# Low parts of the left pieces on VectorE instead of GpSimd, in the down stage of a decoder layer

## The chip, the cores and the metric

The kernel is one program on one core of a Trainium2 chip. The metric is the time of one execution on the device in microseconds, read as the median of several runs. The core has five engines with a queue each, which run their own instructions in order: TensorE (PE: matmuls, and PEld: loads of the weight operand), VectorE (DVE), ScalarE (ACT), GpSimd (POOL), and SyncE (SP), which here only issues DMAs.

## The reference, cut to what matters

The whole is one decoder layer in float32 on 1024 tokens of width 1024: an entry normalisation, two groups of attention heads, an output projection, a normalisation, a SwiGLU feed-forward of width 2816, and a last normalisation. The change touches the last product of the feed-forward, the one with w_down:

```
def swiglu_ffn(h, w_gate_up, w_down):
    gate, up = jnp.split(h @ w_gate_up, 2, axis=-1)
    return (jax.nn.silu(gate) * up) @ w_down
...
        ffn = swiglu_ffn(h, w_gate_up[l], w_down[l])
        h = layer_norm(ALPHA * h + ffn, ln2_g[l], ln2_b[l])
```

## The kernel before, in words

**Precision.** TensorE multiplies in a reduced form of float32. To keep the precision, every operand is split into a high part (a cast, on ScalarE) and a low part (operand minus high part, a subtraction of two tiles in SBUF on VectorE or GpSimd). Each product is then three matmuls: high x high, high x low, low x high. `split_to` (L766 to L769) does one split; its argument `eng` is the engine of the low part.

**The down stage.** The product of the activations (1024 x 2816) with w_down (2816 x 1024) is done as a 2 x 2 block product with seven instead of eight block multiplications, named P1, P5, P2, P3, P6, P7, P4 in the order in which they run. Each block multiplication has 11 steps k of 128 rows (KF = 11), and each step needs one left piece (128 x 512, from `a_dram`, which the stage before has filled with the four blocks and three sums of them) and one right piece (128 x 512, a block of w_down or a sum of blocks). `left_part` (L811) loads a left piece into a tile `ar` and splits it into `ahl`; `right_part` (L816) forms block sums of the right pieces in place (tiles `bq`, L818) and splits into `bhl`, or for P7 and P4 into another `bq`. `down` (L771) multiplies the pair: four blocks of 128 tokens x three matmuls, 12 matmuls in all (L776), into four PSUM tiles `pd`. The tags ahl and bhl have four buffers each, ar eight.

The first four steps of P1 (EARLY, L784) stand apart, run while the stage before is still ending, and split into tiles `w`; the code of the other steps of P1 is the loop over k from 4 to 10, and that of P5, P2, P3, P6, P7, P4 the loop at L868. After a block multiplication VectorE adds the PSUM tiles into the rows `h` (`scaled`, L849, h<-h,pd); P1's result goes through a tile `uu` and is added from there (h<-h,uu). After P6 and P4 the function `one` normalises finished rows and stores them.

**Who does what.** Before the change GpSimd takes the low parts of all left pieces (L768, ahl and, in every other step of P7 and P4, bhl) and one block sum of P3 (L818); VectorE takes the low parts of all right pieces, the other block sums (one in P5, two in P6, L818), and all drains; ScalarE takes all casts (L767).

**What sets the order.** The instructions are put in order by a scheduler, engine by engine, when the program is built; so an instruction may stand well ahead of the place where the code issues it, and the order on each engine is fixed from then on. The loads of the down stage are on SyncE's queue in the order of the code (`Ordered`). The tail of the stage before leaves four more sums on GpSimd (L712 to L715), behind which ScalarE issues stores to `a_dram` (L716 to L718).

Of the kernel before, what the change touches and what calls it, by code (L numbers as in the profile page):

```python
# [74 lines left out]
def layer(ctx: ExitStack, tc: tile.TileContext, x, ln_in, w_sw, w_sb, norm_g,  # L75
          sinks, rel_bias, onehot, w_out, ln1, w_gu, w_down, ln2, out):
    nc = tc.nc
    pe, act, dve, pool = nc.tensor, nc.scalar, nc.vector, nc.gpsimd
# [38 lines left out]
    def ln_stats(xt, n=2):  # L117
        bst = st.tile([P, n, 6], F32, tag=f"bst{n}", name="bst")
        w = D // n
        for i in range(n):  # L120
            dve.bn_stats(out=bst[:, i, :], in_=xt[:, i * w:(i + 1) * w])
        mv = st.tile([P, 2], F32, tag="mv", name="mv")
        dve.bn_aggr(out=mv, in_=bst)
        rstd = st.tile([P, 1], F32, tag="rstd", name="rstd")
        rpow(rstd, mv[:, 1:2], 1.0, LN_EPS)
        return mv[:, 0:1], rstd

    def ln_apply(dst, xt, g, b, fast=False):
        mu, rstd = ln_stats(xt)
        if fast:  # L130
            dve.scalar_tensor_tensor(out=dst, in0=xt, scalar=mu, in1=g, op0=ALU.subtract, op1=ALU.mult)
            for i in range(2):
                h = slice(i * 512, i * 512 + 512)
                dve.scalar_tensor_tensor(out=dst[:, h], in0=dst[:, h], scalar=rstd, in1=b[:, h],
                                         op0=ALU.mult, op1=ALU.add)
            return
        nmu = st.tile([P, 1], F32, tag="nmu", name="nmu")
        dve.tensor_scalar(out=nmu, in0=mu, scalar1=-1.0, scalar2=None, op0=ALU.mult)
        for i in range(2):
            h = slice(i * 512, i * 512 + 512)  # L140
            act.activation(dst[:, h], xt[:, h], AF.Identity, bias=nmu)
            dve.scalar_tensor_tensor(out=dst[:, h], in0=dst[:, h], scalar=rstd, in1=g[:, h],
                                     op0=ALU.mult, op1=ALU.mult)
            pool.tensor_tensor(out=dst[:, h], in0=dst[:, h], in1=b[:, h], op=ALU.add)
# [621 lines left out]
    def split_to(w, src, eng):  # L766
        act.copy(w[:, 0], src)  # L767
        eng.tensor_tensor(out=w[:, 1], in0=src, in1=_f(w[:, 0]), op=ALU.subtract)  # L768
        return w  # L769

    def down(pd, k, a, b, first, end, ts=range(4)):  # L771
        for t in ts:
            tok = slice(t * P, t * P + P)
            n = 0
            for x, y in ((a[:, 0, tok], b[0]), (a[:, 0, tok], b[1]), (a[:, 1, tok], b[0])):
                pe.matmul(pd[t], x, y, start=(first and k == 0 and n == 0),  # L776
                          stop=(end and k == KF - 1 and n == 2), skip_group_check=True)
                n += 1

    def down_banks(tags):  # L780
        return [bps.tile([P, 512], F32, tag=tags[t // 2], name="pd") for t in range(4)]
# [5 lines left out]
    for k in range(EARLY):  # L787
        r = fw.tile([P, 2, 512], F32, tag="gr", bufs=2, name="r")
# [11 lines left out]
    def raw_b(k, i):  # L800
        return bq[k + i // 2 * KF][:, i % 2 * 512:i % 2 * 512 + 512]

    def load_b(k, i):
        h = slice(i % 2 * 512, i % 2 * 512 + 512)
        f = k + i // 2 * KF
        sp.dma_start(raw_b(k, i), w_down[f * P:(f + 1) * P, h])

    def parts(tag, src, eng, pl=dr, bufs=4):
        return split_to(pl.tile([P, 2, 512], F32R, tag=tag, bufs=bufs, name=tag), src, eng)

    def left_part(i, k, tag="ahl"):  # L811
        r = dr.tile([P, 512], F32, tag="ar", bufs=8, name="ar")
        sp.dma_start(r, a_dram[k][:, i])
        return parts(tag, r, pool)

    def right_part(name, k):  # L816
        b11, b12, b21, b22 = (raw_b(k, i) for i in range(4)) if name != "P1" else [raw_b(k, 0)] * 4
        sub = lambda eng, dst, x, y: eng.tensor_tensor(out=dst, in0=x, in1=y, op=ALU.subtract)  # L818
        if name == "P5":
            sub(dve, b11, b12, b11)  # L820
        elif name == "P6":
            sub(dve, b11, b22, b11)
        src = {"P1": b11, "P5": b11, "P6": b11, "P2": b21, "P3": b22, "P7": b12, "P4": b21}[name]
        if name in ("P7", "P4"):
            w = parts("bq", src, dve, *((dr, KF + 1) if name == "P7" else (dn, KF + 2)))
        else:
            w = parts("bhl", src, dve)
        if name == "P3":
            sub(pool, b12, b22, b12)
        elif name == "P6":  # L830
            sub(dve, b21, b21, b11)
        return w[:, 0], w[:, 1]
# [9 lines left out]
    with tc.tile_pool(name="dn", bufs=4, reuse_waits="tile") as dn:  # L842
        bq += [dn.tile([P, D], F32, tag="bq", bufs=KF + 2, name="bq") for k in range(KF)]
        h = [dn.tile([P, D], F32, tag="h", bufs=NT, name="h") for t in range(NT)]
        LEFT = {"P2": 1, "P4": 2, "P5": 3, "P6": 4, "P7": 5, "P3": 6}
        NEEDS = {"P5": (1,), "P2": (2,), "P3": (3,), "P6": (), "P7": (), "P4": ()}

        def scaled(dst, src, c=1.0):
            dve.scalar_tensor_tensor(out=dst, in0=dst, scalar=c, in1=src, op0=ALU.mult, op1=ALU.add)  # L849

        def one(t):
            ot = dn.tile([P, D], F32, tag="ot", bufs=2, name="ot")
            rows = slice(t * P, (t + 1) * P)
            if t < NT - 1:
                ln_apply(ot, h[t], g2, b2)
                nc.sync.dma_start(out[rows, :], ot)
                return
            mu, rstd = ln_stats(h[t], 4)
            for x in (d0, d1):
                dve.scalar_tensor_tensor(out=ot[:, x], in0=h[t][:, x], scalar=mu, in1=g2[:, x],  # L860
                                         op0=ALU.subtract, op1=ALU.mult)
            for x, q in ((d0, act), (d1, nc.sync)):
                dve.scalar_tensor_tensor(out=ot[:, x], in0=ot[:, x], scalar=rstd, in1=b2[:, x],  # L863
                                         op0=ALU.mult, op1=ALU.add)
                q.dma_start(out[rows, x], ot[:, x])

        pt = down_banks(("pp", "tr"))
        for name in ("P5", "P2", "P3", "P6", "P7", "P4"):  # L868
            if name == "P6":
                pz = down_banks(("z", "av"))  # L870
            ps = pt if name in ("P5", "P3") else pz
            first, last, end = name in ("P5", "P6"), name == "P4", name in ("P2", "P4", "P3")
            held = []
            for k in range(KF):
                if name == "P5" and k < EARLY:
                    load_b(k, 0)
                for i in NEEDS[name]:
                    load_b(k, i)
                if name == "P5" and k > KF - 5:
                    for t in (k - KF + 8, k - KF + 4):  # L880
                        sp.dma_start(h[t], h1_dram[t])
                ab = (left_part(LEFT[name], k, "bhl" if name in ("P7", "P4") and k % 2 else "ahl"), right_part(name, k))
                if last and k > 3:
                    held.append((k, *ab))
                else:
                    down(ps, k, *ab, first, end)
            if name == "P3":
                g2 = dn.tile([P, D], F32, tag="g2", bufs=1, name="g2")
                b2 = dn.tile([P, D], F32, tag="b2", bufs=1, name="b2")
                bc_load(g2, ln2[0])  # L890
                bc_load(b2, ln2[1])
            for t in range(4):
                for k, a, b in held:
                    down(ps, k, a, b, first, end, (t,))
                if name == "P5":
                    scaled(h[4 + t][:, d1], ps[t], ALPHA)
                elif name == "P2":
                    scaled(h[t][:, d0], ps[t], ALPHA)
                elif name in ("P3", "P6"):
                    scaled(h[t][:, d1], ps[t])  # L900
                elif name == "P7":
                    scaled(h[4 + t][:, d1], ps[t])
                else:
                    scaled(h[4 + t][:, d0], ps[t])
                if name in ("P6", "P4"):
                    one(t if name == "P6" else 4 + t)
            if name == "P2":
                for t in range(4):
                    scaled(h[t][:, d1], uu[:, t], ALPHA)
                    scaled(h[4 + t][:, d0], uu[:, t], ALPHA)  # L910
                    scaled(h[4 + t][:, d1], uu[:, t])
# [50 lines left out]
```

## Time and profile before

| | us |
|---|---|
| median of 3 runs | 1236.27 |
| lowest and highest run | 1234.16, 1238.58 |
| the profiled execution's own time | 1236.33 |
| its span, first to last instruction | 1234.6 |
| TensorE busy | 1151.2 (93%) |
| VectorE busy | 867.5 (70%) |
| GpSimd busy | 750.0 (61%) |
| ScalarE busy | 570.9 (46%) |
| TensorE's mean granted clock | 0.964 |

The shares are means over the whole layer; the change lies in the last fifth of it, so views of that stretch alone are read below. Times in the rows are microseconds from the span's start. A group's idle time is that of the engine just before the instructions, with the engine whose work ended it.

### The profile page before, as it was taken

The numbers are of one execution on the slowest core, as the hardware profiler recorded it, in microseconds if no ns is written. First come the engines' busy times: TensorE is split into PE (matmuls) and PEld (weight loads), VectorE is DVE, ScalarE is ACT, GpSimd is POOL, SyncE is SP. The second block draws the span as 40 slices with busy tenths as digits, with TensorE's granted clock in tenths as the row PEclk, the third lists the DMA queues.
The fourth block names the chain that finished last, engine by engine and source line by source line (L and its number), as shares of the span: only waits on it lengthen the run. The fifth ranks groups of instructions, "written<-read, shape, count | busy, mean of one in ns | idle before, by whom it ended". The sixth has DMA issues, their size and how long they took to land. (4 is left out here: it accounts for less than half of the span.)

```text
span 1234.6 us, 17707 instructions
## 1 busy us (share of the span) xinstructions
PE 1151.2 (93%) x6246; PEld 990.9 (80%) x6246; DVE 867.5 (70%) x1257; ACT 570.9 (46%) x1224; POOL 750.0 (61%) x682
## 2 busy tenths in 40 slices
PE   5698999999998998977999999999999999979997
PEld 4688999899997886765888888888888888757785
DVE  7885786787889894777765645656456349998645
ACT  4565677767678564233433222332232234425531
POOL 5514344556647877567877656666557455774694
PEclk9798999999999898987999999999999999989998
DMA  7213102020105525134333323333323269643441
GB/s 274 93 55 94 35 23 77 23 66 22 49 18 172 186 99 192 73 121 145 119 128 111 103 76 112 111 111 102 95 94 111 95 218 396 212 137 93 114 134 68
DMA packets 60054, 140.69 MB, mean 114 GB/s; under 512 B 7060, under 2 KB 18877, under 8 KB 59966
## 3 DMA queue, kind: packets, MB, share of 16 engines
q1 hardware_dynamic: 45406, 110.71, 28.1%
q10 hardware_dynamic: 14560, 28.85, 6.1%
q8 instruction: 49, 0.80, 0.3%
q14 instruction: 39, 0.32, 0.1%
HBM read 95.75 MB, written 41.17 MB: 111 GB/s over the span
## 5 line engine op out<-in xcount | busy, mean ns | idle before, releaser
L107 POOL TENSOR_TENSOR w<-s,w 128x512 fp32r<-128x512 f32 x88 | 124.1, 1413 | 119.2 <-ACT w L106 119.2
L154 PE MATMUL pp<-xh,whi 128*128 128x256 f32 x544 | 158.8, 293 | 0.0
L154 PE MATMUL pp<-xh,wlo 128*128 128x256 f32 x544 | 158.2, 291 | 0.0
L154 PE MATMUL pp<-xl,whi 128*128 128x256 f32 x544 | 157.5, 290 | 0.0
L776 PE MATMUL pd<-bhl,ahl 128*128 128x512 f32 x612 | 146.6, 400 | 10.0 <-DVE bhl L768 9.6
L776 PEld LDWEIGHTS pd<-bhl,ahl 128*128 128x128 f32 x612 | 117.0, 193 | 39.4 <-DVE bhl L768 14.9
L106 ACT CAST w<-s 128x512 fp32r<-128x512 f32 x88 | 54.4, 622 | 202.7 <-PE pgu L703 118.9
L768 POOL TENSOR_TENSOR ahl<-ar,ahl 128x512 fp32r<-128x512 f32 x63 | 92.6, 1477 | 59.1 <-ACT ahl L767 57.0
L735 DVE TENSOR_TENSOR t<-t,pgu 128x512 f32<-128x512 f32 x88 | 60.1, 683 | 96.6 <-PE pgu L703 96.2
L433 POOL TENSOR_TENSOR s<-s,s 128x127 f32<-128x127 f32 (+2 forms) x96 | 92.6, 969 | 37.7 <-DVE s L429 33.3
L154 PEld LDWEIGHTS pp<-xh,wlo 128*128 128x128 f32 x544 | 106.6, 196 | 1.2
L154 PEld LDWEIGHTS pp<-xl,whi 128*128 128x128 f32 x544 | 106.6, 196 | 1.0
L154 PEld LDWEIGHTS pp<-xh,whi 128*128 128x128 f32 x544 | 106.5, 196 | 0.6
L429 DVE TENSOR_TENSOR_SCAN s<-s,brk 128x128 f32<-128x128 f32 (+1 forms) x64 | 74.7, 1174 | 11.2 <-ACT s L420 10.6
L374 POOL TENSOR_TENSOR L<-L,rd 128x512 f32<-128x512 f32 (+1 forms) x32 | 30.9, 989 | 81.5 <-DVE rd L372 63.9
L110 ACT CAST at<-tra 128x256 fp32r<-128x256 f32 (+1 forms) x160 | 55.5, 356 | 52.7 <-DVE at L111 30.9
L768 DVE TENSOR_TENSOR bhl<-bq,bhl 128x512 fp32r<-128x512 f32 x51 | 67.8, 1338 | 8.2 <-ACT bhl L767 7.9
L111 DVE TENSOR_TENSOR at<-tra,at 128x256 fp32r<-128x256 f32 (+1 forms) x160 | 58.5, 383 | 15.8 <-ACT at L110 14.6
L107 POOL TENSOR_TENSOR w<-gr,w 128x512 fp32r<-128x512 f32 x44 | 61.2, 1405 | 2.3 <-ACT w L106 2.3
L703 PE MATMUL pgu<-B11h,w 128*128 128x512 f32 x176 | 59.1, 398 | 1.4 <-ACT w L106 1.4
L767 ACT CAST ahl<-ar 128x512 fp32r<-128x512 f32 x63 | 38.9, 619 | 43.0 <-POOL ahl L768 17.1
L703 PE MATMUL pgu<-T4h,w 128*128 128x512 f32 x176 | 57.9, 390 | 0.0
(222 smaller groups left out, 3351.2 us busy)
## 6 DMA issues: line engine op xcount, KB each, us to landing
ar<-a_dram SPq DMA_DIRECT2D x73, 256.0 KB, 2.9
a_dram<-act ACTq DMA_DIRECT2D x33, 512.0 KB, 2.6
gr<-in_w_gu SPq DMA_DIRECT2D x24, 512.0 KB, 3.6
ur<-in_w_gu SPq DMA_DIRECT2D x23, 512.0 KB, 3.5
bq<-in_w_down SPq DMA_DIRECT2D x44, 256.0 KB, 4.3
raw<-in_w_sb SPq DMA_DIRECT2D x12, 512.0 KB, 3.4
h_dram<-x ACTq DMA_DIRECT2D x8, 512.0 KB, 3.3
m<-o_dram SPq DMA_DIRECT2D x32, 128.0 KB, 3.0
```

What stands on the lines that cost most here:

```text
L106: act.copy(hi, raw)
L107: pool.tensor_tensor(out=lo, in0=raw, in1=_f(hi), op=ALU.subtract)
L110: act.copy(hi, ps)
L111: dve.tensor_tensor(out=lo, in0=ps, in1=_f(hi), op=ALU.subtract)
L154: pe.matmul(ps, a, b, start=(i == 0), stop=(i == n - 1))
L429: dve.tensor_tensor_scan(s2[:, 0:w][:, ::-1], s2[:, 0:w][:, ::-1], brk[:, 512 - w:][:, ::-1] if last else zero.broadcast_to([P, w]), 1.0 i ...
L433: pool.tensor_tensor(out=s1[:, 0:m], in0=s1[:, 0:m], in1=s2[:, 1:m + 1], op=ALU.mult)
L703: pe.matmul(ps, a, b, start=(start and n == 0), stop=(stop and n == 11), skip_group_check=True)
L735: add = lambda out, x: dve.tensor_tensor(out=out, in0=x, in1=ps, op=ALU.add)
L767: act.copy(w[:, 0], src)
L768: eng.tensor_tensor(out=w[:, 1], in0=src, in1=_f(w[:, 0]), op=ALU.subtract)
L776: pe.matmul(pd[t], x, y, start=(first and k == 0 and n == 0), stop=(end and k == KF - 1 and n == 2), skip_group_check=True)
```

## The change

In P1 (steps 4 to 10), P5, P2, P3 and P6 the low parts of the left pieces are made on VectorE instead of GpSimd, by a new argument of `left_part`; P7 and P4 name GpSimd and stay as they were, and so do the first four steps of P1. The block sum of P3 moves to VectorE too. Nothing else changes: the same values are computed, in the same tiles.

```diff
-    def left_part(i, k, tag="ahl"):
+    def left_part(i, k, tag="ahl", eng=dve):
         r = dr.tile([P, 512], F32, tag="ar", bufs=8, name="ar")
         sp.dma_start(r, a_dram[k][:, i])
-        return parts(tag, r, pool)
+        return parts(tag, r, eng)
...
         if name == "P3":
-            sub(pool, b12, b22, b12)
+            sub(dve, b12, b22, b12)
         elif name == "P6":
             sub(dve, b21, b21, b11)
...
-                ab = (left_part(LEFT[name], k, "bhl" if name in ("P7", "P4") and k % 2 else "ahl"), right_part(name, k))
+                ab = (left_part(LEFT[name], k, "bhl" if name in ("P7", "P4") and k % 2 else "ahl",
+                                pool if name in ("P7", "P4") else dve), right_part(name, k))
```

The order on GpSimd before, from the last sums of the stage before (L712) on into P3:

```order
L712 TENSOR_TENSOR act<-act 128x512
L714 TENSOR_TENSOR act<-act 128x512
L768 TENSOR_TENSOR ahl<-ar,ahl 128x512
L713 TENSOR_TENSOR act<-act 128x512
L768 TENSOR_TENSOR ahl<-ar,ahl 128x512 x2
L715 TENSOR_TENSOR act<-act 128x512
L768 TENSOR_TENSOR ahl<-ar,ahl 128x512 x21
L818 TENSOR_TENSOR bq<-bq 128x512
L768 TENSOR_TENSOR ahl<-ar,ahl 128x512
L818 TENSOR_TENSOR bq<-bq 128x512 x2
```

The same place on GpSimd after the change; the rows of L768 are now those of P7, whose left pieces use ahl and bhl in turn:

```order
L712 TENSOR_TENSOR act<-act 128x512
L714 TENSOR_TENSOR act<-act 128x512
L713 TENSOR_TENSOR act<-act 128x512
L715 TENSOR_TENSOR act<-act 128x512
L768 TENSOR_TENSOR ahl<-ar,ahl 128x512
L768 TENSOR_TENSOR bhl<-ar,bhl 128x512
L768 TENSOR_TENSOR ahl<-ar,ahl 128x512
```

Between L715 and P7 nothing is left on GpSimd.

The order on VectorE before, from the low part of the right piece of P2's step k = 7 (bhl_10662) to that of its step k = 10 (bhl_10725); rows of L818 are block sums of P6, and L768 into a bq is a right part of P4, made ahead:

```order
L768 TENSOR_TENSOR bhl_10662<-bq_10235,bhl_10662 128x512
L818 TENSOR_TENSOR bq_10063<-bq_10231,bq_10063 128x512
L768 TENSOR_TENSOR bq_11577<-bq_10229,bq_11577 128x512
L818 TENSOR_TENSOR bq_10230<-bq_10230,bq_10062 128x512
L768 TENSOR_TENSOR bhl_10683<-bq_10236,bhl_10683 128x512
L818 TENSOR_TENSOR bq_10064<-bq_10232,bq_10064 128x512
L818 TENSOR_TENSOR bq_10231<-bq_10231,bq_10063 128x512
L768 TENSOR_TENSOR bhl_10704<-bq_10237,bhl_10704 128x512
L818 TENSOR_TENSOR bq_10232<-bq_10232,bq_10064 128x512
L818 TENSOR_TENSOR bq_10065<-bq_10233,bq_10065 128x512
L768 TENSOR_TENSOR bhl_10725<-bq_10238,bhl_10725 128x512
```

The same place on VectorE after the change, from the left and right low parts of P2's step k = 7 (ahl_10659, bhl_10662) to those of its step k = 8, with the rows just ahead; x2 is P6's sum and P3's, one behind the other:

```order
L818 TENSOR_TENSOR bq_10228<-bq_10228,bq_10060 128x512
L768 TENSOR_TENSOR bq_11333<-bq_10060,bq_11333 128x512
L818 TENSOR_TENSOR bq_10061<-bq_10229,bq_10061 128x512 x2
L768 TENSOR_TENSOR ahl_10659<-ar_10657,ahl_10659 128x512
L818 TENSOR_TENSOR bq_10062<-bq_10230,bq_10062 128x512 x2
L768 TENSOR_TENSOR bhl_10662<-bq_10235,bhl_10662 128x512
L768 TENSOR_TENSOR bq_11557<-bq_10228,bq_11557 128x512
L818 TENSOR_TENSOR bq_10063<-bq_10231,bq_10063 128x512 x2
L818 TENSOR_TENSOR bq_10229<-bq_10229,bq_10061 128x512
L768 TENSOR_TENSOR ahl_10680<-ar_10678,ahl_10680 128x512
L768 TENSOR_TENSOR bhl_10683<-bq_10236,bhl_10683 128x512
```

The left low parts stand among VectorE's rows now, each next to its right one, and P3's sums beside P6's.

## Rows read from the trace of the kernel before

**Rows 1.** Windows: length, engines' busy time and count, TensorE's clock, DMA share, GB/s.

```profile
1060.00:1090.00 30.00, 24.93 (x101) 19.56 (x100) 29.71 (x24) 10.51 (x19) 25.79 (x17) 0.94 0.46 147
1090.00:1120.00 30.00, 25.28 (x94) 18.82 (x94) 29.93 (x36) 11.54 (x21) 16.55 (x11) 0.89 0.38 114
```

**Rows 2.** TensorE in order of time: start, length, line, tiles, count, idle before.

```profile
1008.72 68.39 PE L776 MATMUL pd<-bhl,ahl 128*128 128x512 f32 x301
1078.00 3.01 PE L776 MATMUL pd<-bhl,ahl 128*128 128x512 f32 x12 [0.89 <-DVE bhl L768]
1084.75 4.61 PE L776 MATMUL pd<-bhl,ahl 128*128 128x512 f32 x12 [3.73 <-DVE bhl L768]
1089.80 8.63 PE L776 MATMUL pd<-bhl,ahl 128*128 128x512 f32 x36 [0.44 <-DVE bhl L768]
1100.53 4.28 PE L776 MATMUL pd<-bhl,ahl 128*128 128x512 f32 x12 [2.10 <-DVE bhl L768]
1107.28 57.98 PE L776 MATMUL pd<-bhl,ahl 128*128 128x512 f32 x239 [2.47 <-DVE bhl L768]
...
1224.79 0.84 PE L776 MATMUL pd<-bq,ahl 128*128 128x512 f32 x3
```

**Rows 3.** Waits of the down stage: who for whom, total, times, longest.

```profile
POOL ahl L768 <- ACT ahl L767: 57.0, 32, 5.5
...
PEld pd L776 <- DVE bhl L768: 14.9, 11, 4.2
...
PE pd L776 <- DVE bhl L768: 9.6, 5, 3.7
```

**Rows 4.** Short windows of TensorE alone: length, busy time, clock, DMA share, GB/s.

```profile
1080.00:1085.00 5.00, 1.27 (x6) 0.99 0.61 186
1085.00:1090.00 5.00, 4.56 (x13) 0.67 0.43 132
...
1100.00:1105.00 5.00, 4.28 (x12) 0.70 0.33 102
```

**Rows 5.** VectorE in order of time, while GpSimd works.

```profile
1081.28 1.75 DVE L818 TENSOR_TENSOR bq<-bq 128x512 f32<-128x512 f32 x1
1082.95 1.74 DVE L768 TENSOR_TENSOR bhl<-bq,bhl 128x512 fp32r<-128x512 f32 x1
```

**Rows 6.** GpSimd in order of time, at the same place.

```profile
1080.77 1.71 POOL L768 TENSOR_TENSOR ahl<-ar,ahl 128x512 fp32r<-128x512 f32 x1
1082.43 1.71 POOL L818 TENSOR_TENSOR bq<-bq 128x512 f32<-128x512 f32 x1
```

**Rows 7.** GpSimd in order of time: two rows behind long idle times.

```profile
1046.27 1.62 POOL L768 TENSOR_TENSOR ahl<-ar,ahl 128x512 fp32r<-128x512 f32 x1 [2.48 <-ACT ahl L767]
...
1096.43 1.83 POOL L768 TENSOR_TENSOR ahl<-ar,ahl 128x512 fp32r<-128x512 f32 x1 [5.54 <-ACT ahl L767]
```

**Rows 8.** VectorE in order of time, while GpSimd is idle.

```profile
1044.26 0.68 DVE L818 TENSOR_TENSOR bq<-bq 128x512 f32<-128x512 f32 x1
...
1046.67 1.77 DVE L768 TENSOR_TENSOR bhl<-bq,bhl 128x512 fp32r<-128x512 f32 x1
...
1091.96 0.68 DVE L768 TENSOR_TENSOR bhl<-bq,bhl 128x512 fp32r<-128x512 f32 x1
...
1097.02 1.78 DVE L818 TENSOR_TENSOR bq<-bq 128x512 f32<-128x512 f32 x1
```

**Rows 9.** One window of TensorE alone, with the DMA share.

```profile
1027.00:1057.00 30.00, 30.00 (x134) 1.00 1.03 402
```

**Rows 10.** Groups by line and shape: count, busy time, mean ns, idle before.

```profile
L768 POOL TENSOR_TENSOR ahl<-ar,ahl 128x512 fp32r<-128x512 f32 x63 | 92.6, 1477 | 59.1 <-ACT ahl L767 57.0 <-issue 1.9
L818 POOL TENSOR_TENSOR bq<-bq 128x512 f32<-128x512 f32 x11 | 18.9, 1729 | 0.0
```

**Rows 11.** ScalarE in order of time: the two casts of one pair.

```profile
1036.16 0.62 ACT L767 CAST ahl<-ar 128x512 fp32r<-128x512 f32 x1 [1.58 <-POOL ahl L768]
1036.69 0.62 ACT L767 CAST bhl<-bq 128x512 fp32r<-128x512 f32 x1
```

## The prediction

> **What bounds the kernel now.** I read the table of windows first, then the order of time on TensorE, then the waits, then VectorE and GpSimd side by side. A full window of 30 us holds 30.00 us of TensorE work; the two windows from 1060 to 1120 us hold 24.93 and 25.28 at a granted clock of 0.94 and 0.89, and in both VectorE is busy 29.71 and 29.93 of 30 us [rows 1]. So in this stretch VectorE sets the pace; it is the part of the down stage in which the products P2 and P3 are multiplied.
>
> The price of it is read from TensorE's order of time [rows 2]. From 1008.72 us it runs 301 matmuls in 68.39 us without a gap: (68.39 - 0.39) / 300 = 0.2267 us a matmul (0.39 us is the last one's own length), 2.72 us for the 12 matmuls of one k step of one block product (a "pair" below: one left piece, one right piece). Then it stops five times, 0.89 + 3.73 + 0.44 + 2.10 + 2.47 = 9.63 us, each time for a right low part (bhl) that VectorE writes in L768; the table of waits says the same twice, for the weight load and for the matmul [rows 3]. From 1008.72 us there are 612 matmuls with bhl and 144 + 120 with bq, 876 in all. At 0.2267 us each they would end at 1008.72 + 875 x 0.2267 + 0.39 = 1207.47 us; they end at 1224.79 + 0.84 = 1225.63. The loss is **18.16 us**: 9.63 us of waiting, and 8.5 us mostly of slow clock behind the waits: after the stops of 3.73 and 2.10 us the granted clock of five-microsecond windows reads 0.67 and 0.70 (between the levels 2.4 and 1.2 GHz), while after the stop of 0.89 us it read 0.99 [rows 4]. 18.16 us is also the most that this change can give: TensorE is gapless before 1077 us, and the 9.0 us from 1225.63 to the end of the span are the last rows' normalisation, which the change leaves alone.
>
> **Why VectorE is slow.** Where GpSimd works at the same time, the two engines go in step: VectorE starts an operation at 1081.28 and 1082.95 us, each 1.75 us long, GpSimd at 1080.77 and 1082.43, each 1.71 us long, so one on each engine per 1.67 us [rows 5, 6]; in the stretch around it the step is 1.70. Where GpSimd is idle (5.54 us before 1096.43, 2.48 us before 1046.27) [rows 7], VectorE does eight operations of the same size from 1091.96 to 1097.02, 0.63 us each, and four from 1044.26 to 1046.67, 0.60 us each [rows 8]. The second place lies in a window in which the DMA engines are busy all the time (share 1.03, 402 GB/s) [rows 9], and ScalarE casts in both places; so the slow step goes with GpSimd and with nothing else that I see.
>
> **The change part by part.** GpSimd loses 51 left low parts (7 of P1, whose first four k steps keep the old code, and 11 each of P5, P2, P3, P6) at 1.477 us and 11 block sums of P3 at 1.729 us [rows 10], 94 us of its busy time. VectorE gains 62 operations of 128x512. They are subtractions of two tiles in SBUF like the ones it does already, so I price them by the steps of [rows 8], 0.60 to 0.63 us, value 0.605, near the lower end, because four operations in a row start exactly 0.60 us apart there and the 0.63 has a step in it in which GpSimd was just about to start: 62 x 0.605 = 37.5 us more work. Against that, every operation that was in step with a GpSimd one falls from 1.70 to 0.605 us. One operation on each engine took 1.70 us; both on VectorE take 1.21. The upper bound for the price is the 1.70 us step itself, if GpSimd were not its cause (third rival); below 0.60 there is no row.
>
> Does VectorE then keep up? The order of instructions puts 177 VectorE operations between the last pair of P1 and the last of P6, drains and sums of uu among them: 4.0 for each of 44 pairs, 2.43 us against TensorE's 2.72. But it also puts P6's sums and P4's right parts forward into the end of P2 and the start of P3. Counting all VectorE operations of the new order up to each pair (pair 0 is P1's k = 4), the densest stretch is pair 25 to 32 (P2 from k = 7 to P3 k = 3): 47 operations, 28.4 us, against 8 x 2.72 = 21.8 us on TensorE. What covers it is the lead. The buffers of ahl and bhl are four deep, so ScalarE casts pair n when TensorE has released pair n - 4; its two casts stand 0.53 us apart, 0.62 us each [rows 11], and VectorE's low part adds 0.6, so a pair is ready some 1.9 us after that release and 3 x 2.72 - 1.9 = 6.2 us before TensorE wants it. Two block sums stand in the queue just ahead of pair 24, so I take 6.0 there. Over the dense stretch 28.4 - 21.8 = 6.6 us go, so TensorE waits 0.6 us once; the next four pairs have 19 operations, 11.5 us against 10.9, another 0.6 us. At 0.60 us an operation the two waits sum to 0.9 us, at 0.63 to 2.9. From pair 37 on the count is below TensorE's need (28 operations, 16.9 us, for seven pairs of 19.0) and the lead comes back.
>
> Edits at no cost: the four sums L712 to L715 of the last spill now stand together on GpSimd, so the DMAs that ScalarE issues behind them, and the casts behind those, go no later. In P1 VectorE has 15 operations, 9.1 us, in the 19 us of TensorE's seven pairs. If these covers were gone, TensorE's gapless start [rows 2] would get the same waits as P3 has. In P7 and P4 GpSimd keeps its 22 left parts as now.
>
> **The sum.** 1236.33 us (profiled execution: span 1234.6 and 1.7 around it) - 18.16 + 1.2 = 1219.4 us. That execution is 0.06 us from the median of the three runs, so the sum stands for the median too.
>
> **Rivals.**
> *First, the dense stretch is worse than counted.* If an operation on VectorE takes 0.65 us on average (hand-overs with ScalarE between them), pairs 25 to 32 take 30.6 us against 21.8 + 6.0 of cover, 2.8 us of waiting, and pairs 33 to 36 12.4 against 10.9, 1.5 more. Waits of this size cost clock as well: now 9.63 us of waiting cost 18.16, a factor of 1.9. 4.3 x 1.9 = 8.2, so 1236.33 - 18.16 + 8.2 = 1226.4 us; at 0.70 us, 7.5 x 1.9 gives 1232. For it: the 0.63 of one place. Against it: 0.60 in the other.
> *Second, a wait takes the place of the one removed.* GpSimd's left parts now wait 57.0 us, in 32 waits, for ScalarE's casts [rows 3]; these waits move into VectorE's queue, and block sums, drains and right parts stand behind them. Most are the harmless wait for a released buffer. If they ate the lead whole, the dense stretch would cost 6.6 + 0.6 = 7.2 us, times 1.9 = 13.7: 1231.9, about where 0.3% from now begins.
> *Third, slower: VectorE is simply full.* It is busy 99% from 1060 to 1120 us, and if its step there is not GpSimd's doing, it stays: 24 + 36 operations in 59.6 us [rows 1], 0.99 us each. Then the 113 operations of the new order from pair 25 to the end of P6 take 112 us from 1068 (TensorE's start of pair 24 at 1074 less 6.0), and P6 ends at 1068 + 112 + 2.7 = 1182.7 where it now ends at 1165.1, so 1236.33 + 17.6 = 1253.9 us. It decides from (1162.4 - 1068) / 113 = 0.84 us an operation on (1162.4: the start of P6's last pair now). Against it stand the twelve quick operations of [rows 8]. The Trainium skill, in Perfetto Trace Analysis, section Optimizing Scalar/DVE Operations, speaks for this rival: with a saturated VectorE it suggests giving work to ScalarE or even GpSimd, the opposite of this change. The same section warns that the two share a read port to SBUF, so that shifting work between them might not help; the trace agrees with the warning, 1.70 us for a pair side by side.
>
> **How the numbers follow.** A measurement of this kernel can tell about 0.3%, 3.7 us, from no change. Forecast (1216 to 1223): 0.76. First rival, 1223 to 1232: 0.13. Second, about 1232 and just above: 0.05. Third, slower: 0.04. Something that I don't see, without a gain or a loss: 0.02. Faster 0.90, same 0.06, slower 0.04. The range goes from 1216 (nothing waits, and 0.2% of scatter, as the three runs show) to 1227, the first rival at 0.65 us, and leaves out less than 2 in 10.
>
> **What would show it.** Right: bhl and ahl on VectorE mean 0.7 to 0.8 us, GpSimd idle from about 1011 us to the end of P6, TensorE from 1008.7 to about 1148 us with waits below 3 us in all, first near 1096, and a granted clock near 1.00; P7 begins about 1148 instead of 1165. Wrong: VectorE operations above 0.8 us with GpSimd idle (third rival), or TensorE stops of over 2 us near 1096 and 1108 with a clock that falls after them (first), or VectorE idle for ScalarE's casts while TensorE stands (second).

## The result

| | before | after |
|---|---|---|
| median of 6 runs, us | 1235.96 | 1215.68 |
| profiled execution's span, us | 1234.6 | 1215.1 |
| down stage: first matmul with bhl to end of the last, us | 216.91 | 199.03 |
| VectorE busy, us | 867.5 | 852.9 |
| GpSimd busy, us | 750.0 | 655.0 |

The changed kernel takes 0.9842 of the time before, 95% interval 0.9824 to 0.986: faster, by 19.5 us give or take 2.2. The forecast was 1219.4 us, in a range from 1216 to 1227; the median lies 3.7 us below the forecast and 0.3 us below the low end. VectorE has 62 operations more and is busy for less time. (One run of before, at 2270.08 us, was disturbed; the median hardly feels it and the ratio leaves it out.)

The two windows of [rows 1], read from the kernel after: length, then busy time and count of TensorE, its weight loads, VectorE, ScalarE and GpSimd, then TensorE's clock, DMA share, GB/s.

```profile
1060.00:1090.00 30.00, 30.00 (x134) 24.86 (x133) 30.00 (x51) 14.74 (x28) 0.00 (x0) 1.00 0.57 176
1090.00:1120.00 30.00, 29.98 (x133) 24.50 (x132) 30.00 (x51) 18.00 (x33) 0.00 (x0) 1.00 0.50 141
```

VectorE is still busy all the time, 30.00 of 30 us; but it now does 51 operations in each window where it did 24 and 36. TensorE is full, at a granted clock of 1.00, and GpSimd does nothing. A busy share alone would have shown no difference on VectorE.

TensorE in order of time, answering to [rows 2] (start, length, line, tiles, count):

```profile
1007.13 139.20 PE L776 MATMUL pd<-bhl,ahl 128*128 128x512 f32 x612
1146.16 0.84 PE L776 MATMUL pd<-bq,ahl 128*128 128x512 f32 x3
...
1205.32 0.84 PE L776 MATMUL pd<-bq,ahl 128*128 128x512 f32 x3
```

The five stops are gone: all 612 matmuls with bhl are one piece. 611 x 0.2267 + 0.39 would be 138.9 us; 0.3 us is lost. The weight loads show where, as the one wait in the whole stretch, after 436 = 36 x 12 + 4 of them:

```profile
1006.91 98.79 PEld L776 LDWEIGHTS pd<-bhl,ahl 128*128 128x128 f32 x436
1106.14 39.77 PEld L776 LDWEIGHTS pd<-bhl,ahl 128*128 128x128 f32 x176 [0.44 <-DVE bhl L768]
```

VectorE in order of time, from the densest part of its queue, and GpSimd on both sides of its idle time:

```profile
1073.55 0.68 DVE L768 TENSOR_TENSOR ahl<-ar,ahl 128x512 fp32r<-128x512 f32 x1
1074.15 0.68 DVE L768 TENSOR_TENSOR bhl<-bq,bhl 128x512 fp32r<-128x512 f32 x1
1074.75 1.88 DVE L818 TENSOR_TENSOR bq<-bq 128x512 f32<-128x512 f32 x3
1076.56 0.68 DVE L768 TENSOR_TENSOR ahl<-ar,ahl 128x512 fp32r<-128x512 f32 x1
```

```profile
1007.95 1.62 POOL L715 TENSOR_TENSOR act<-act 128x512 f32<-128x512 f32 x1
1138.90 1.29 POOL L768 TENSOR_TENSOR ahl<-ar,ahl 128x512 fp32r<-128x512 f32 x1 [129.33 <-ACT ahl L767]
```

Five operations from 1073.55 to 1076.56 us: 0.60 us each, as in [rows 8]. By groups (count, busy time, mean ns, idle before), low parts and sums on VectorE are all near 0.7 us long, where bhl had a mean of 1338 ns before. The first row is from the kernel before, the others from the kernel after:

```profile
L768 DVE TENSOR_TENSOR bhl<-bq,bhl 128x512 fp32r<-128x512 f32 x51 | 67.8, 1338 | 8.2 <-ACT bhl L767 7.9 <-PE pd L776 0.3
...
L768 DVE TENSOR_TENSOR ahl<-ar,ahl 128x512 fp32r<-128x512 f32 x51 | 37.1, 728 | 8.6 <-ACT ahl L767 8.5
L768 DVE TENSOR_TENSOR bhl<-bq,bhl 128x512 fp32r<-128x512 f32 x51 | 37.0, 726 | 1.9 <-ACT bhl L767 1.9
...
L818 DVE TENSOR_TENSOR bq<-bq 128x512 f32<-128x512 f32 x44 | 28.7, 682 | 1.0 <-DMA bq<-in_w_down 0.9
```

### The profile page after: what moved, and what is told of

Read it like the earlier page. It is cut to its first block, busy times and chain, and to the rows that moved or that the text cites. A ratio compares the mean times of both kernels' runs of the same rounds, so it can differ in the third digit from the quotient of the medians.

```text
span 1215.1 us, 17655 instructions
## 1 busy us (share of the span) xinstructions
PE 1138.8 (94%) x6246; PEld 984.6 (81%) x6246; DVE 852.9 (70%) x1319; ACT 572.5 (47%) x1224; POOL 655.0 (54%) x620
## 3 DMA queue, kind: packets, MB, share of 16 engines
q1 hardware_dynamic: 45406, 110.71, 28.4%
## 5 line engine op out<-in xcount | busy, mean ns | idle before, releaser
L776 PE MATMUL pd<-bhl,ahl 128*128 128x512 f32 x612 | 139.2, 389 | 0.0
L768 POOL TENSOR_TENSOR ahl<-ar,ahl 128x512 fp32r<-128x512 f32 x12 | 16.2, 1354 | 134.8 <-ACT ahl L767 134.7
L703 PE MATMUL pgu<-B22h,w 128*128 128x512 f32 x176 | 57.8, 389 | 0.0
```

Source lines behind the costliest of these rows:

```text
L703: pe.matmul(ps, a, b, start=(start and n == 0), stop=(stop and n == 11), skip_group_check=True)
```

## The experiments

My theory: GpSimd's own work slows VectorE while both run, and that, in the dense stretch from P2 to P3, is what TensorE waited for. Rivals: the hand-over of each left piece through a third engine and its queue; only one of the two parts of the change; and VectorE's number of operations alone. "Stage" below is the time from the first matmul with bhl to the end of the last matmul in the run's profile; it leaves out the scatter of the earlier stages.

One thing changed besides the two parts. The scheduler also put TensorE's matmuls in another order: in the kernel before, 48 of the 51 pairs with bhl wait for the right low part at their second matmul (the first stop of [rows 2] comes after 301 = 25 x 12 + 1 of them); in the changed kernel pairs 25 to 45 wait for it at their fifth or a later one. That alone can move a need by 3 x 0.2267 = 0.7 us, once and not once a pair, since VectorE's queue goes on at its own pace; with the factor of 1.9 that the forecast took for the clock, an estimate of 1.3 us. It is not the gain: e1, e2, e3, e5, e10 and e11 wait at the third or a later matmul in all or nearly all pairs of the dense stretch too, and are slower than the changed kernel by 4 to 30 us in the stage, while e8 has the old order and is 11 us faster than before.

| run | what differs | ratio to before (95%) | median us | stage us |
|---|---|---|---|---|
| after | | 0.9842 (0.9824 to 0.986) | 1215.68 | 199.03 |
| e1 | P3's sums back on GpSimd | 0.9897 (0.9882 to 0.9912) | 1221.85 | 203.26 |
| e2 | left parts back on GpSimd | 0.9929 (0.9905 to 0.9954) | 1226.86 | 212.11 |
| e6 | left parts on VectorE in P2, P3 alone | 0.9835 (0.9803 to 0.9867) | 1215.45 | 199.07 |
| e7 | left parts on VectorE in P7, P4 too | 0.9833 (0.9816 to 0.9851) | 1215.69 | 199.04 |
| e5 | 51 idle operations more, on VectorE | 0.9926 (0.9905 to 0.9946) | 1227.28 | 210.98 |
| e3 | 51 on GpSimd, two reads each | 1.0049 (1.0029 to 1.0068) | 1241.36 | 225.13 |
| e10 | 51 on GpSimd, one read each | 0.9952 (0.9927 to 0.9976) | 1229.50 | 210.80 |
| e4 | 51 on GpSimd, no read | 0.9858 (0.9843 to 0.9873) | 1217.06 | 198.72 |
| e11 | 51 on GpSimd, on a tile of its own | 1.0093 (1.0064 to 1.0122) | 1245.00 | 228.87 |
| e8 | before, left low parts by memset | 0.9898 (0.9877 to 0.9918) | 1223.94 | 205.80 |
| e9 | e8 with P3's sums on VectorE | 0.9843 (0.9824 to 0.9863) | 1214.04 | 198.72 |

### The two parts apart (e1, e2)

```diff
# e1, against after
-            sub(dve, b12, b22, b12)
+            sub(pool, b12, b22, b12)
# e2, against after
-    def left_part(i, k, tag="ahl", eng=dve):
+    def left_part(i, k, tag="ahl", eng=pool):
...
-                                pool if name in ("P7", "P4") else dve), right_part(name, k))
+                                pool), right_part(name, k))
```

> The changed kernel with P3's eleven block sums back on GpSimd; the left low parts stay on VectorE. My theory (side by side, one operation on each engine takes 1.70 us, both on VectorE 1.21): VectorE loses 11 operations of 0.60 us and eleven of its other operations go from 0.60 to 1.70 us, net 11 x (1.10 - 0.60) = 5.5 us in the dense stretch, which has no lead left: 1219 to 1226 us, with TensorE waiting again near 1090 to 1110 us. Rival (the left low parts are the whole effect and the sums nothing): 1215.7 us, and VectorE less busy by 6.6 us.

> The kernel before with the one block sum of P3 moved to VectorE and nothing else: the left low parts are on GpSimd. My theory: eleven of the 62 side-by-side steps go, 11 x (1.10 - 0.60) = 5.5 us of VectorE's time in the stretch that sets the pace, and with the clock up to twice that: 1226 to 1232 us. Rival (only the sums in the dense stretch matter, the left low parts are hidden): 1216 to 1219 us. Rival (only the left parts matter): 1236 us.

Both came out inside what the theory gave, and outside all three rivals. In the stage the left parts alone are worth 216.91 - 203.26 = 13.7 us, the sums alone 4.8, and both 17.9: they nearly add up.

The way there was not quite the one expected. In e1 the theory wanted eleven steps of 1.70 us on VectorE; the trace has, beside the eleven sums, five operations that are longer by 1.1 us and four by 0.5 us, 7.5 us in all, against 6.6 us of sums that left VectorE. Three of the five come before the parts of pair 24 are ready (at 1067.78 us, TensorE at 1071.12), so the lead there is 3.3 us instead of 6.0; of the other sums one stood for 16.32 us on GpSimd and slowed VectorE not at all (last section). So e1's number fits in part by luck. In e2 one of TensorE's stops is not for VectorE but for a left part that GpSimd itself finished late (TensorE, then GpSimd):

```profile
1086.90 6.21 PE L776 MATMUL pd<-bhl,ahl 128*128 128x512 f32 x19 [3.00 <-POOL ahl L768]
```

```profile
1076.13 10.71 POOL L768 TENSOR_TENSOR ahl<-ar,ahl 128x512 fp32r<-128x512 f32 x1 [4.21 <-ACT ahl L767]
```

So VectorE holds up GpSimd too (more in the last section), and not only GpSimd VectorE. Groups of e2 show which operations of VectorE suffer:

```profile
L849 DVE SCALAR_TENSOR_TENSOR h<-h,pd 128x512 f32<-128x512 f32 x24 | 15.8, 678 | 22.7 <-PE pd L776 22.7
L849 DVE SCALAR_TENSOR_TENSOR h<-h,uu 128x512 f32<-128x512 f32 x12 | 14.3, 1214 | 0.0
```

The two are the same instruction on the same shape. The one with an input in PSUM has its quick length, 678 ns, the one with both inputs in SBUF 1214. Both run beside GpSimd: 18 of the 24 with a PSUM input overlap a GpSimd instruction that reads by more than 0.3 us, and none of them is longer than 0.69 us. So what counts is what VectorE reads.

### Which products (e6, e7)

```diff
# e6, against after (with eng=pool as the default)
-                                pool if name in ("P7", "P4") else dve), right_part(name, k))
+                                dve if name in ("P2", "P3") else pool), right_part(name, k))
# e7, against after
-                                pool if name in ("P7", "P4") else dve), right_part(name, k))
+                                dve), right_part(name, k))
```

> The changed kernel with the left low parts on VectorE in P2 and P3 alone, and on GpSimd in P1, P5 and P6; P3's sums on VectorE. My theory (only the dense stretch, P2 to P3, sets the pace): P1 and P5 have cover for the slow steps as before the change, P6 has 47 operations for pairs 37 to 50, 36 at 0.60 and eleven at 1.70 us, 40 us against 38, so little is lost: 1216 to 1223 us. Rival (each product counts alike): 22 of 51 left parts and the sums give about half of the gain, 1225 to 1228 us.

> The changed kernel with the left low parts of P7 and P4 on VectorE as well, 73 - 51 = 22 more operations. My theory: TensorE has no gap in P7 and P4 with the parts on GpSimd, so nothing is to be gained: 1215.7 us within 2.5. If it is faster, the last normalisations got their GpSimd steps sooner; if slower, VectorE's normalisations of the first rows stand in front of pairs that TensorE waits for, at 0.7 to 1.1 us each, 3 to 8 us.

22 of the 51 left parts, with the sums, give the whole gain. In e6 bhl still has a mean of 1051 ns, and TensorE does not care, since in P1, P5 and P6 the slow steps have cover:

```profile
1003.33 139.24 PE L776 MATMUL pd<-bhl,ahl 128*128 128x512 f32 x612
```

e7 changes nothing either way, as expected: with TensorE gapless in this stage, nothing that an engine beside it does faster there is worth anything. No version is faster than the changed kernel beyond the intervals: what is left in this stage is 0.3 us.

### Is it GpSimd's work, or the hand-over? (e8, e9)

```diff
# e8, against before, in left_part; e9 has besides P3's sums on VectorE
-        return parts(tag, r, pool)
+        if tag == "bhl" or i in (2, 5):
+            return parts(tag, r, pool)
+        w = dr.tile([P, 2, 512], F32R, tag=tag, bufs=4, name=tag)
+        act.copy(w[:, 0], r)
+        pool.memset(_f(w[:, 1]), 0.0)
+        return w
```

> The kernel before, but GpSimd fills the 51 left low parts of P1 (k from 4), P5, P2, P3 and P6 with zeros by a memset instead of the subtraction: this leaves those low parts out of the sum. The chain of engines and the waits for it are those of before, P3's sums stay on GpSimd, but the left parts read nothing from SBUF. If reading is what collides: VectorE's bhl falls from 1.34 to about 0.8 us and TensorE hardly waits, 1217 to 1223 us. If any work of GpSimd in SBUF collides, in proportion to its length: 1222 to 1236 us with bhl near 1 us or above. If the hand-over through GpSimd is what cost, 1233 to 1238 us.

> The kernel before with two edits: the left low parts of P1 (k from 4), P5, P2, P3 and P6 are filled with zeros by a memset on GpSimd (this leaves those low parts out of the sum), and P3's block sum is on VectorE. No instruction of GpSimd reads SBUF from the last spill to P7, but every left piece still passes through GpSimd's queue. If GpSimd's reads are the whole cause: TensorE without waits, 1214 to 1218 us, bhl at 0.70 to 0.75 us. If the hand-over through GpSimd's queue has a price of its own (the run with memset and P3's sums on GpSimd came to 1223.9 us, 2 above the run with the sums alone on GpSimd): 1219 to 1224 us.

e9 is the cleanest run of the study. Each left piece still passes through GpSimd, VectorE's queue is nearly that of e2, and the stage takes 198.72 us, without a wait; the changed kernel's 199.03 have their one wait more:

```profile
1006.12 138.88 PE L776 MATMUL pd<-bhl,ahl 128*128 128x512 f32 x612
```

The way through GpSimd's queue to TensorE costs nothing when GpSimd does not read. One part of the hand-over is not tested by this: e8's expectation says that the waits are those of before, but the memset needs no cast of ScalarE. In e9 it waits 46 times for TensorE to release a buffer, 99.2 us, and never for a cast, where before the subtraction waited 57.0 us for casts [rows 3]. That GpSimd's reads cost VectorE time with no hand-over at all is shown further down (e3, e11).

e8 lies 1 us above the first of its expectations in time, while bhl has the length that it names (793 ns). I had misjudged what stays in it: the eleven sums of P3 on GpSimd, which read. VectorE and GpSimd there (VectorE above):

```profile
1070.61 1.77 DVE L768 TENSOR_TENSOR bq<-bq 128x512 fp32r<-128x512 f32 x1
1072.31 1.79 DVE L823 TENSOR_TENSOR bq<-bq 128x512 f32<-128x512 f32 x1
```

```profile
1068.85 2.99 POOL L823 TENSOR_TENSOR bq<-bq 128x512 f32<-128x512 f32 x2
1071.78 0.53 POOL L818 MEMSET ahl<- 128x512 f32 x1
1072.27 1.29 POOL L823 TENSOR_TENSOR bq<-bq 128x512 f32<-128x512 f32 x1
```

e9 differs from e8 by these sums alone, and by the order that the scheduler then gives. It is 7.1 us faster in the stage and 0.55% of before's time, 6.8 us, by the ratios.

### The same work put beside VectorE (e3, e4, e5, e10, e11)

```diff
# against after, in left_part
-        return parts(tag, r, eng)
+        w = parts(tag, r, eng)
+        if eng is dve:
+            pool.tensor_tensor(out=r, in0=r, in1=r, op=ALU.subtract)    # e3
+            pool.memset(r, 0.0)                                         # e4 in its place
+            dve.tensor_tensor(out=r, in0=r, in1=r, op=ALU.subtract)     # e5 in its place
+            pool.tensor_scalar(out=r, in0=r, scalar1=2.0, scalar2=None, op0=ALU.mult)  # e10
+            pool.tensor_tensor(out=scr, in0=scr, in1=scr, op=ALU.mult)  # e11, scr a tile of its own, ar with 7 buffers
+        return w
```

> The changed kernel, and behind each of the 51 left low parts that moved one more subtraction of 128x512 on GpSimd, of the raw left tile from itself into itself, whose result nobody reads: GpSimd works as before the change, but TensorE, VectorE and ScalarE wait for nothing that it makes. My theory (the work of GpSimd itself slows VectorE): 51 steps of VectorE go from 0.60 to about 1.70 us, 56 us more, of which some 20 to 30 are not covered: 1240 to 1270 us, slower than before the change, and VectorE's mean for bhl near 1.3 us. Rival (what cost before was the hand-over through a third engine and its queue, not its work): 1215.7 us within 2.

> The same as the run before it in the list, with a memset of the raw left tile on GpSimd in place of the subtraction: at the same place, with the same waits, but it writes SBUF only and reads nothing. Theory one (GpSimd's reads collide with VectorE's operations of two SBUF inputs): no slow steps, bhl near 0.73 us, 1215.7 us within 3. Theory two (any access of GpSimd to SBUF collides): VectorE's operations side by side with a memset are longer by about its length, and the time lies between 1220 and 1265 us.

> The changed kernel, and behind each of the 51 left low parts that moved one more subtraction of 128x512 on VectorE, of the raw left tile from itself into itself, whose result nobody reads. My theory (an operation costs VectorE 0.60 us, and the dense stretch has no lead left): 243 operations to the end of P6 instead of 192; from pair 6 to 36 160 of them, 96.6 us against 81.6 on TensorE with 6 of lead, so 9 to 12 us of waiting, with the clock up to twice that: 1225 to 1238 us. It should cost less than the same operation on GpSimd does. Rival (VectorE still has room): 1215.7 us.

> The changed kernel, and behind each of the 51 left low parts one GpSimd instruction that reads one tile and writes it back (the raw left tile times two), whose result nobody reads. With a subtraction (two reads) in this place the time was 1241.4 us, with a memset (no read) 1217.1. If a single read collides as two do: each instruction holds up one VectorE operation for most of its own length; at a length of 0.7 to 1.0 us that is about 20 to 40 us on VectorE, and 1222 to 1238 us. If only instructions with two reads collide: 1215 to 1219 us.

> The changed kernel with 51 multiplications of 128x512 on GpSimd on a tile of its own (no other instruction touches it), one issued with each left low part that moved but tied to nothing; to make room for the tile, ar has seven buffers instead of eight. The two earlier runs with extra GpSimd work held up loads too, since each instruction kept a raw tile from being reloaded; here nothing can wait for GpSimd, so what is lost is lost through VectorE's speed alone. GpSimd runs them from about 1006 us on, in P1, P5 and the start of P2. If the two engines alternate as before the change (1.70 us a step), VectorE does one operation per 1.7 us up to about 1095 us, where TensorE needs 1.2 operations per us, and TensorE loses 20 to 45 us: 1235 to 1260 us. If VectorE's unbroken row of operations holds GpSimd off, as for 15 us in the run with P3's sums on GpSimd, little is lost: 1216 to 1222 us with GpSimd instructions of several us. If GpSimd's work costs VectorE nothing, 1215.7 us with GpSimd instructions of 1.3 us.

The memset of e4 takes 527 ns on GpSimd beside a VectorE that goes on in steps of 0.60 us; its interval overlaps that of the changed kernel, and its stage is as short. VectorE, then GpSimd:

```profile
1066.73 0.69 DVE L768 TENSOR_TENSOR ahl<-ar,ahl 128x512 fp32r<-128x512 f32 x1
1067.34 0.69 DVE L768 TENSOR_TENSOR bhl<-bq,bhl 128x512 fp32r<-128x512 f32 x1
1067.94 0.68 DVE L821 TENSOR_TENSOR bq<-bq 128x512 f32<-128x512 f32 x1
```

```profile
1067.53 0.53 POOL L816 MEMSET ar<- 128x512 f32 x1 [1.92 <-DVE ahl L768]
```

In e10, whose GpSimd instruction reads one tile, VectorE's operations beside it are longer, by 0.4 us here (VectorE, then GpSimd):

```profile
1068.83 0.68 DVE L768 TENSOR_TENSOR bhl<-bq,bhl 128x512 fp32r<-128x512 f32 x1
1069.43 1.09 DVE L821 TENSOR_TENSOR bq<-bq 128x512 f32<-128x512 f32 x1
```

```profile
1069.05 1.81 POOL L816 TENSOR_SCALAR ar<-ar 128x512 f32<-128x512 f32 x1 [1.01 <-DVE ahl L768]
```

So writing alone does not collide; reading does, with one read (e10) as with two (e3). The Trainium skill says so in SBUF — State Buffer, section Who interferes with whom: a VectorE instruction with two SBUF inputs contends with a GpSimd instruction that reads SBUF, not with one that only writes it. e4, e9 and the two groups of e2 agree with it.

e3 lost more than its own argument explains. VectorE's groups grew by about 0.67 us per GpSimd instruction (34 us in all), less than the 1.1 I had reckoned, and e5's 51 operations on VectorE itself weigh nearly the same, 51 x 0.60 = 31 us; still e3 cost 26 us and e5 12. By the trace the rest came through the loads: a raw tile could not be loaded again before the GpSimd instruction on it was done, and SyncE's queue stood behind it (the GpSimd instruction that began at 1083.32 us stood for 9.80). SyncE's waits from 1060 to 1110 us in e3, and VectorE without work for lack of a load:

```profile
SPq L71 <- POOL ar L816: 36.8, 10, 13.2
```

```profile
1096.57 1.29 DVE L821 TENSOR_TENSOR bq<-bq 128x512 f32<-128x512 f32 x2 [4.34 <-DMA bq<-in_w_down]
```

e10 has the same flaw, so the prices of e3 and e10 are not those of the collision alone; that a read collides is shown, how a second read adds to it is not. e11 takes the flaw away, since nothing needs what GpSimd makes there, and VectorE waits for no load in it, though ar has one buffer less. (Four of the multiplications stand in GpSimd's queue ahead of the last sum of the stage before.) GpSimd runs 47 multiplications in one row, and VectorE (above) follows in step:

```profile
1030.38 1.52 DVE L768 TENSOR_TENSOR bhl<-bq,bhl 128x512 fp32r<-128x512 f32 x1
1031.83 1.53 DVE L824 TENSOR_TENSOR bq<-bq 128x512 f32<-128x512 f32 x1
1033.28 1.53 DVE L768 TENSOR_TENSOR ahl<-ar,ahl 128x512 fp32r<-128x512 f32 x1
```

```profile
1015.40 68.03 POOL L819 TENSOR_TENSOR scr<-scr 128x512 f32<-128x512 f32 x47
```

68.03 / 47 = 1.447 us, and VectorE starts an operation every 1.45 us: one each, in turn. The windows of e11 (columns as above) show it end when GpSimd's row ends at 1083 us:

```profile
1030.00:1060.00 30.00, 20.55 (x79) 14.95 (x78) 30.00 (x22) 9.50 (x17) 28.43 (x21) 0.94 0.69 257
...
1090.00:1120.00 30.00, 30.00 (x134) 24.86 (x133) 30.00 (x50) 15.46 (x28) 0.00 (x0) 1.00 0.63 203
```

22 operations of VectorE in 30 us beside GpSimd, 50 without, and busy 30.00 us in both. By the ratios the run is 2.5% of before's time, some 31 us, slower than the changed kernel (29.8 us of it in the stage), and it is slower than the kernel before, by work on which nothing depends. That settles the direction of cause. e5, within its expectation, sets the price of an operation on VectorE at 0.60 us; TensorE's first stop in it is at pair 32, in the dense stretch, but its longest, 2.96 us, is at pair 42, in P6.

## Why the prediction came out as it did

**The bound and its loss.** Right. The 18.16 us read off TensorE's order of time were what there was to gain in the stage, and the stage gave 216.91 - 199.03 = 17.88 of them. The clock came back with the waits, without anything done for it: 1.00 in both windows.

**The price of an operation.** Right: from the end of pair 24's low parts (next start 1066.32 us) to the end of pair 32's (next start 1094.60) VectorE does 47 operations in 28.28 us, 0.602 each, against 28.4 us in the forecast. This term carried the whole sum, and it came from two short places where GpSimd happened to pause.

**The remaining waits.** Mis-sized: 1.2 us forecast, 0.3 measured. The lead at pair 24 was the 6.0 us assumed (ready at 1066.40, TensorE at 1072.41), and pair 32's right part was late as counted: written at 1094.68, while the pair began at 1007.13 + 32 x 2.72 = 1094.17. But the step took the pair as needed at its first matmul. In the code the first of the three multiplies high by high, and the second reads the right low part. In the changed program the scheduler has put four matmuls high by high ahead in these pairs, so only the fifth reads it, 4 x 0.2267 = 0.91 us after the pair begins. So pair 32 was in time (needed at 1095.08 us), and pair 36, written at 1106.08 and needed at 1105.05 + 0.91 = 1105.96, was late by little: the 0.44 us on the weight loads shown above. By the same times of VectorE the two pairs would have waited about 0.5 us each at the first matmul, as forecast, and about 0.3 and 0.5 at the second (estimates). That the waits were smaller is luck: nobody forecast TensorE's new order, and the text ahead of the prediction, which says that nothing else changes, leaves it out.

**The rest of the kernel.** 0.9 us of the 3.7 by which the median lies below the forecast are these waits. In the profiled pair another 1.59 us came before the down stage, which begins at 1008.72 us before and 1007.13 after. That is scatter: TensorE's 501st matmul starts at 102.87 and 101.35 us, long before any instruction differs, and over the profiles of all versions its first matmul with bhl lies between 1003.33 and 1009.31 us. The low end of the range took 0.2% from three runs for this, which was too little: 6 us are 0.5%. Before's median less the 17.88 us of the stage is 1218.1 us, inside the measured interval (0.9824 to 0.986 of 1235.96, 1214.2 to 1218.7 us); the rest of the gap can't be told from scatter.

**The rivals.** The first (0.65 us or more an operation) did not come: 0.602. The second (GpSimd's 57 us of waiting move into VectorE's queue) moved 8.5 us of it, 14 waits for ScalarE's casts of ahl, none of which TensorE felt; e9 shows that the path from GpSimd on to TensorE had no price of its own. The third (VectorE is simply full) rested on VectorE's 99%; e11 and e9 show that this 99% was in good part waiting for GpSimd's reads, booked as work. The advice of the Trainium skill that was cited for it, to relieve a saturated VectorE, even towards GpSimd (Perfetto Trace Analysis, section Optimizing Scalar/DVE Operations), would have pointed the wrong way here. The warning there, that shifting work between the two might not help, agrees with e1 and e2, where work put back on GpSimd cost 4.2 and 13.1 us of the stage; the other direction helped.

## What to carry to other kernels

Before an engine is called full, compare the mean length of its operations with the length of the same operation while its neighbour is idle; a share of 99% at twice the length is not the engine's own work. A GpSimd instruction that reads SBUF is not free help beside a VectorE that reads two SBUF tiles: here both on VectorE took 1.20 us and one on each 1.70, so such work belongs on VectorE where the stretch is tight, and may stay on GpSimd where there is cover. To find the tight stretch, count the operations of the in-order queue pair by pair against the consumer's pace, with the lead that the buffers allow, and check in the program as built, not in the code alone, which matmul of a pair reads the late operand first.

## What the runs showed of the hardware that was not expected

The turn-taking is not always one for one. In e1 GpSimd had a single sum to do, after a pause, beside an unbroken row of two-input operations on VectorE, and it stood for 16.32 us (the shortest of its kind there took 1.46; the profile's spans on GpSimd are rough):

```profile
1075.89 16.32 POOL L818 TENSOR_TENSOR bq<-bq 128x512 f32<-128x512 f32 x1 [4.06 <-DMA bq<-in_w_down]
```

VectorE went on in steps of 0.60 us all that time, until it came to operations with only one input in SBUF:

```profile
1090.37 0.68 DVE L818 TENSOR_TENSOR bq<-bq 128x512 f32<-128x512 f32 x1
1090.97 1.27 DVE L849 SCALAR_TENSOR_TENSOR h<-h,pd 128x512 f32<-128x512 f32 x2
1092.17 0.68 DVE L818 TENSOR_TENSOR bq<-bq 128x512 f32<-128x512 f32 x1
```

GpSimd's instruction ended at 1092.21 us, about the length of one instruction after the first of these began. In e3 and e10 single instructions stood for up to 13.4 and 13.3 us, in e2 for the 10.7 us shown above. In all runs together nine instructions of GpSimd that read stood for over 7 us, and each of them ended 0.9 to 1.5 us after the first break in VectorE's row of two-input operations: an operation with at most one input in SBUF, or an idle time, of which 0.11 us (e5) was enough. Eight of the nine began after GpSimd had paused for 3.4 us or more; one, in e10, had no pause before it. In e11, with GpSimd's queue full before, the two alternated for 68 us and neither was shut out. What decides between the two patterns was not tried and stays open. It matters for what is placed on GpSimd: an instruction that something waits for may come not 0.4 but 15 us late.
